# Attention: value sums and output projection exchange two PSUM banks with every group of heads

## The chip, the cores and the metric

The kernel runs on one core of one Trainium2 chip. The metric is the device time of one execution in microseconds (us). The engines are named as in the profile: PE is TensorE's matmul side, PEld its weight loads, DVE VectorE, ACT ScalarE, POOL GpSimd, SP the engine that issues DMAs. Each engine carries out its own instructions in the order of its queue.

## The reference, cut to what matters

One layer of a hybrid decoder: 1024 tokens, width 1024, float32. The normed input is projected; 8 heads of sparse attention in 2 groups and 4 heads of a gated recurrence follow; their outputs lie side by side and go through one output projection, which is added to the residual. A feed-forward block ends the layer. The change lies in the attention and the output projection that is woven into it:

```python
o = g[..., 0:1] * o_cmp + g[..., 1:2] * o_sel + g[..., 2:3] * o_win
...
mix = jnp.concatenate([o_nsa.astype(x.dtype), o_hgrn.astype(x.dtype)], axis=-1)
x = x + mix @ w_out[l]
```

`o_cmp`, `o_sel` and `o_win` are softmax(q k) v over compressed blocks, selected blocks and a window of 512 tokens. With 16 blocks of 64 tokens and 16 to be selected, the kernel takes all causal keys for `o_sel`.

## The kernel before

Attention goes through 8 blocks of 128 queries (`qb`), each with 2 groups of 4 heads (`g`), each with 2 branches (`b`: 0 all causal keys, 1 the window): 32 units. A unit has a scoring part and a value part, and the loop issues the scoring of one unit ahead of the values of the unit before it.

- `score`: for each of 4 heads, PE makes q k into a bank (L839 and L840 for the high and the low part of q, L842 for the mask). DVE takes the negated maximum (L847), ACT the exponential with its sum (L848), DVE the reciprocal of the sum (L849), and POOL multiplies by it and by the gate (L850), into `pbig`.
- `values`: for each block of 128 keys, PE transposes the 4 heads' weights (4 of L861) into a bank `ps_t`, ACT copies it as the high part `ph` (L863), DVE makes the low part (L864), and two matmuls of 512 columns, L865 with the high and L866 with the low part, add to the bank `o` of the group. Both units of a group add to one `o`.
- `finish`, after the second unit of a group, adds the compressed branch (L872 to L879) and reads `o` out: ACT L885 and L886 into `fold`, DVE L887 and L888 into `qtok`. From then on the bank is free.
- `prep` makes the queries of the next block ready: POOL writes them scaled (L775), PE transposes them (L781), ACT and DVE split them (L784, L785), and the compressed branch is scored (L790, L795).

The output projection is spread between the units. Each of its 32 tiles of 128 tokens x 512 columns needs 12 matmuls of 512 columns (L118 to L120) for one half of the inputs, `hgrn_out` for the recurrence's half and `nsa_out` for the attention's; DVE L497 adds the bank to `x1`, and the bank is free. A counter `load` decides after which unit the next tile is issued: the first one (`FILL` 6.5) comes at the fourth unit.

PSUM has 8 banks. Here 2 hold `ps_t`, 4 hold scores, and the last two are `a0` and `a1`: `o` always takes `a0` (`bank_o`), the projection always `a1` (`bank_f`). A tile that takes a bank waits until the reads of the tile before it in that bank are done.

The program text isn't the order on the engines: when the kernel is built, a scheduler lays each engine's instructions in an order by its own estimate of durations, within the dependences. A projection tile whose bank and data are ready is so spread, matmul by matmul, over places in PE's queue far ahead of where the text has it.

Of the kernel before, what the change touches and what calls it, by code (L numbers as in the profile page):

```python
# [8 lines left out]
F32 = mybir.dt.float32  # L9
# [9 lines left out]
P = 128  # L19
# [29 lines left out]
def hybrid_layer(ctx: ExitStack, tc: tile.TileContext, x, x_t, par, w_in, k_norm, pos_k, pos_v,  # L49
# [9 lines left out]
    ps = ctx.enter_context(tc.tile_pool(name="ps", bufs=1, space=PSUM))  # L59
# [45 lines left out]
    def rpage():  # L105
        return raw.tile([P, 1024], F32, name="rpage", tag="r")
# [392 lines left out]
    def mixhl():  # L499
        return rpage().bitcast(F32R).rearrange("p (two n) -> p two n", two=2)  # L500

    def bank_f():
        return ps.tile([P, 512], F32, name="a1", tag="a1", bufs=1)

    mixed = {}

# [7 lines left out]
    def hgrn_out(t, n, bank=bank_f):  # L514
        if n == 0 and t:
            mixed[t] = mix_parts(gmix[:, :, t * P:(t + 1) * P])
        out_tile(w_b, t, n, *mixed[t], bank)
# [212 lines left out]
    with tc.tile_pool(name="at", bufs=1) as at:  # L730
        g_bc = at.tile([P, D], F32, name="g_bc")
        nc.sync.dma_start(g_bc, norm_ffn[0:1, :].broadcast_to([P, D]))
        def nsa_out(t, n):
            if n == 0:
                mixed[t] = mix_parts(qtok[:, t].rearrange("p (c n) -> p c n", c=4))
            out_tile(w_t, t, n, *mixed[t], bank_f)
            if n == 1:
                nc.sync.dma_start(x1_d[t * P:(t + 1) * P, :], x1[:, t, :])
                rs2 = norm_stats(x1[:, t, :], rpage())
                if t == NT - 1:  # L740
                    g_last = rpage()
                    nc.sync.dma_start(g_last, norm_ffn[0:1, :].broadcast_to([P, D]))
                    V.scalar_tensor_tensor(x1[:, t, :], x1[:, t, :], rs2, g_last, op0=OP.mult, op1=OP.mult)
                    return
                A.activation(x1[:, t, :], x1[:, t, :], AF.Copy, scale=rs2)
                G.tensor_tensor(x1[:, t, :], x1[:, t, :], g_bc, op=OP.mult)
                if t >= 4:
                    G.tensor_tensor(x1[:, t, 0:512], x1[:, t, 0:512], x1[:, t - 4, 0:512], op=OP.subtract)
# [15 lines left out]
            return turns[1][:, 512 * (turns[0] - 2):512 * (turns[0] - 1)]  # L764

        def bank_o():
            return ps.tile([P, 512], F32, name="a0", tag="a0", bufs=1)

        def segs(n):
            return [(0, n)] if n <= 512 else [(0, n // 2), (n // 2, n // 2)]  # L770
# [127 lines left out]
        for i, u in enumerate(units + [None]):  # L898
# [8 lines left out]
            if pending:  # L907
                free[0] = i >= len(units) - 1
                (qb, g, b), kb0, wts = pending
                if b == 0:  # L910
                    o_bank[g] = bank_o()
                values(qb, g, b, kb0, wts, o_bank[g])
                if b == 1:
                    finish(qb, g, prepped[qb][1], o_bank[g])
                    if g == 1:
                        nq += [(qb, 0), (qb, 1)]
# [369 lines left out]
```

## Time and profile before

| what | us |
|---|---|
| median of 3 runs (1403.95, 1405.82, 1405.95) | 1405.82 |
| the profiled execution: its own time | 1406.47 |
| its span, first to last instruction | 1404.6 |
| PE busy in the span | 1371.6 |
| DVE busy | 1048.0 |
| ACT busy | 596.5 |
| POOL busy | 392.1 |

The attention with its woven-in projection lies between 394 and 742 us of the span. The profiled execution took 1.9 us more than its span, and its time is 0.65 us above the median. A busy PE need not be at its peak: a matmul that has begun and is held up counts as busy, so the distance from one start to the next tells more than busy time does. PEclk is the granted clock as a share of 2.4 GHz; the other level is 1.2 GHz, 0.5.

### The profile page before, as it was taken

The numbers are of one execution on the slowest core, as the hardware profiler recorded it, in microseconds if no ns is written. First come the engines' busy times: TensorE is split into PE (matmuls) and PEld (weight loads), VectorE is DVE, ScalarE is ACT, GpSimd is POOL, SyncE is SP. The second block draws the span as 40 slices with busy tenths as digits, with TensorE's granted clock in tenths as the row PEclk, the third lists the DMA queues.
The fourth block names the chain that finished last, engine by engine and source line by source line (L and its number), as shares of the span: only waits on it lengthen the run. The fifth ranks groups of instructions, "written<-read, shape, count | busy, mean of one in ns | idle before, by whom it ended". The sixth has DMA issues, their size and how long they took to land.

```text
span 1404.6 us, 19716 instructions
## 1 busy us (share of the span) xinstructions
PE 1371.6 (98%) x7092; PEld 1129.5 (80%) x7092; DVE 1048.0 (75%) x1893; ACT 596.5 (42%) x1153; POOL 392.1 (28%) x341
## 2 busy tenths in 40 slices
PE   9999999999999999999998999999999999999998
PEld 7888888989977777777776888888888888887787
DVE  5317888626788888888877888888888887689764
ACT  7323333323446666566654433333333333443332
POOL 0001111010044442344436433233233230158400
PEclk9999999999999999999999999999999999999999
DMA  8411110111220001000003333333333328887521
GB/s 324 127 45 31 31 31 28 54 31 46 94 88 1 1 1 61 31 16 31 16 16 105 96 101 97 112 98 113 113 112 99 106 98 294 327 300 269 171 97 55
DMA packets 108769, 135.72 MB, mean 97 GB/s; under 512 B 6112, under 2 KB 63872, under 8 KB 108672
## 3 DMA queue, kind: packets, MB, share of 16 engines
q1 hardware_dynamic: 108672, 134.46, 28.7%
q8 instruction: 56, 0.92, 0.3%
q14 instruction: 41, 0.34, 0.1%
HBM read 105.87 MB, written 28.57 MB: 96 GB/s over the span
## 4 chain that ended last, share of the span: by engine, by line
PE 82%; DVE 12%; ACT 2%; issue 2%; POOL 1%; DMA 1%; SPq 0%; ACTq 0%; POOLq 0%; DVEq 0%
PE bank L118 9%; PE bank L119 9%; PE bank L120 9%; PE a L118 8%; PE a L120 8%; PE a L119 8%; PE ps_t L119 4%; PE ps_t L120 4%; PE ps_t L118 4%; PE ps_t L861 3%; PE a L865 2%; DVE wop L112 2%; PE a L866 2%; PE ps_t L375 1%; PE ps_s L839 1%
## 5 line engine op out<-in xcount | busy, mean ns | idle before, releaser
L850 POOL TENSOR_SCALAR pbig<-pbig,den,gates 128x640 f32<-128x640 f32 (+7 forms) x128 | 103.9, 816 | 166.9 <-DVE den L849 146.9
L111 ACT ACTIVATE wop<-rpage 128x512 fp32r<-128x512 f32 x132 | 82.7, 630 | 156.9 <-PE bank L120 70.7
L112 DVE TENSOR_TENSOR wop<-rpage,wop 128x512 fp32r<-128x512 f32 x132 | 100.7, 765 | 14.6 <-ACT wop L111 12.7
L864 DVE TENSOR_TENSOR ph<-ps_t,ph 128x512 fp32r<-128x512 f32 x126 | 84.3, 683 | 18.5 <-ACT ph L863 17.6
L863 ACT ACTIVATE ph<-ps_t 128x512 fp32r<-128x512 f32 x126 | 72.7, 596 | 49.6 <-PE ps_t L861 39.7
L381 POOL TENSOR_TENSOR kp<-kp,fp 128x256 f32<-128x256 f32 x28 | 20.3, 725 | 232.8 <-PE bank L358 181.3
L861 PE MATMUL ps_t<-ident,pbig 128*128 128x128 f32 x504 | 78.7, 275 | 2.1 <-POOL pbig L850 2.1
L112 DVE TENSOR_TENSOR wop<-act_a,wop 128x512 fp32r<-128x512 f32 x48 | 46.8, 976 | 33.1 <-ACT wop L111 33.1
L861 PEld LDWEIGHTS ps_t<-ident,pbig 128*128 128x128 f32 x504 | 61.0, 141 | 11.9 <-POOL pbig L850 3.2
L1012 POOL TENSOR_TENSOR tmp<-tmp,rpage 128x512 f32<-128x512 f32 x21 | 31.3, 1488 | 140.6 <-DVE wop L112 140.6
L112 DVE TENSOR_TENSOR wlo<-wraw,whi 128x1024 fp32r<-128x1024 f32 (+2 forms) x27 | 32.0, 1188 | 46.0 <-PE a L120 19.3
L848 ACT ACTIVATE pbig<-ps_s,nm 128x640 f32<-128x640 f32 (+3 forms) x64 | 55.9, 875 | 24.1 <-DVE nm L847 19.0
L111 ACT ACTIVATE wop<-act_a 128x512 fp32r<-128x512 f32 x48 | 30.3, 631 | 82.8 <-PE bank L120 58.0
L118 PE MATMUL bank<-wop 128*128 128x512 f32 x165 | 65.3, 396 | 0.1
L119 PE MATMUL bank<-wop 128*128 128x512 f32 x165 | 65.2, 395 | 0.0
L120 PE MATMUL bank<-wop 128*128 128x512 f32 x165 | 65.1, 394 | 0.0
L847 DVE TENSOR_REDUCE nm<-ps_s 128x1 f32<-128x640 f32 (+3 forms) x64 | 58.1, 913 | 4.7 <-PE ps_s L842 3.0
L865 PE MATMUL a<-ph,kv 128*128 128x512 f32 x132 | 58.8, 445 | 2.2 <-ACT ph L863 1.4
L866 PE MATMUL a<-ph,kv 128*128 128x512 f32 x132 | 57.5, 436 | 2.9 <-DVE ph L864 1.8
L112 DVE TENSOR_TENSOR wop<-tmp,wop 128x512 fp32r<-128x512 f32 x42 | 43.6, 1039 | 20.6 <-ACT wop L111 19.9
L972 POOL TENSOR_TENSOR tmp<-rpage 128x512 f32<-128x512 f32 x20 | 26.1, 1306 | 115.2 <-DMA rpage<-in_w_gate_up_dram 115.2
L111 ACT ACTIVATE wop<-tmp 128x512 fp32r<-128x512 f32 x42 | 26.6, 633 | 70.2 <-POOL tmp L1012 37.5
(458 smaller groups left out, 4454.2 us busy)
## 6 DMA issues: line engine op xcount, KB each, us to landing
rpage<-in_w_gate_up_dram SPq DMA_DIRECT2D x86, 256.0 KB, 3.1
raws<-in_w_down_dram SPq DMA_DIRECT2D x35, 512.0 KB, 7.5
act_a<-act_d SPq DMA_DIRECT2D x12, 1024.0 KB, 6.4
act_d<-as SPq DMA_DIRECT2D x33, 256.0 KB, 2.2
act_e<-act_d SPq DMA_DIRECT2D x6, 1024.0 KB, 7.6
act_d<-tmp SPq DMA_DIRECT2D x22, 256.0 KB, 2.1
act_d<-th SPq DMA_DIRECT2D x22, 256.0 KB, 2.1
xn<-in_x_dram SPq DMA_DIRECT2D x8, 512.0 KB, 5.5
```

The costliest lines, as they stand in the source:

```text
L111: A.activation(hi, src, AF.Copy)
L112: V.tensor_tensor(lo, src, hi.bitcast(F32), op=OP.subtract)
L118: PE.matmul(o, ah, bh, start=first, stop=False, skip_group_check=chained)
L119: PE.matmul(o, ah, bl, start=False, stop=False, skip_group_check=chained)
L120: PE.matmul(o, al, bh, start=False, stop=last, skip_group_check=chained)
L847: V.tensor_reduce(nm, sv, axis=AX.XY, op=OP.max, negate=True)
L850: G.tensor_scalar(pp, pp, den, gates[:, qb, h * 3 + 1 + b:h * 3 + 2 + b], op0=OP.mult, op1=OP.mult)
L861: PE.transpose(pt[:, r * P:(r + 1) * P], wts[r][:, c0:c0 + P], ident)
L863: A.activation(ph[:, 0], pt, AF.Copy)
L864: V.tensor_tensor(ph[:, 1], pt, ph[:, 0].bitcast(F32), op=OP.subtract)
L865: PE.matmul(o, vst[b][:, kb, g, :], ph[:, 0], start=b == 0 and kb == kb0, stop=False)
L866: PE.matmul(o, vst[b][:, kb, g, :], ph[:, 1], start=False, stop=False)
```

## The change

`bank_o` now takes `a1` for the first group, `a0` for the second, and so on in turn; `bank_f` takes whichever of the two the latest group doesn't have, which is the bank of the group before.

```diff
+    side = [0]
+
     def bank_f():
-        return ps.tile([P, 512], F32, name="a1", tag="a1", bufs=1)
+
+        k = 1 - side[0]
+        return ps.tile([P, 512], F32, name=f"a{k}", tag=f"a{k}", bufs=1)
...
         def bank_o():
-            return ps.tile([P, 512], F32, name="a0", tag="a0", bufs=1)
+            side[0] ^= 1
+            return ps.tile([P, 512], F32, name=f"a{side[0]}", tag=f"a{side[0]}", bufs=1)
```

The same instructions run on every engine; their order changes on PE, DVE, ACT and POOL from the first unit of the attention on, and no longer after the attention. SP's order is the same. In the new text lines from 506 to 767 are 4 higher and later ones 5 higher: L790 of before is L795, L781 is L786, L839 is L844, L850 is L855, L775 is L780, L865 is L870.

PE at the first unit, before. `a1_3764` is the first projection tile that is woven in, `ps_t_3463` and `ps_t_3471` are the first queries' transpositions, `bank_3479` the compressed scores, `bank_3508` to `bank_3538` the four heads of the first unit:

```order
L781 MATMUL ps_t_3463<-ident_73,rpage_3461 128x128 x4
L118 MATMUL a1_3764<-whi_3327,rpage_3761 128x512
L781 MATMUL ps_t_3471<-ident_73,rpage_3461 128x128 x4
L119 MATMUL a1_3764<-wlo_3328,rpage_3761 128x512
...
L842 MATMUL bank_3528<-cmask_90,identb_78 128x128
L118 MATMUL a1_3764<-whi_3333,rpage_3761 128x512
L119 MATMUL a1_3764<-wlo_3334,rpage_3761 128x512
L120 MATMUL a1_3764<-whi_3333,rpage_3761 128x512
L118 MATMUL a1_3764<-whi_3339,rpage_3761 128x512
L119 MATMUL a1_3764<-wlo_3340,rpage_3761 128x512
L839 MATMUL bank_3538<-kv2_2683,q_3468 128x256
```

The same place with the change:

```order
L786 MATMUL ps_t_3463<-ident_73,rpage_3461 128x128 x4
L786 MATMUL ps_t_3471<-ident_73,rpage_3461 128x128 x4
L800 MATMUL bank_3479<-kc_st_91,q_3468 128x64
L844 MATMUL bank_3508<-kv2_2683,q_3468 128x256
...
L847 MATMUL bank_3528<-cmask_90,identb_78 128x128
L844 MATMUL bank_3538<-kv2_2683,q_3468 128x256
```

No projection matmul stands there any more. The tile now follows the end of the first group, whose sum is `a1_3588` (PE, with the change; `ps_t_3666` and `ps_t_3674` are the queries of the second block, `bank_3740` a score of the first, `bank_3778` and `bank_3788` scores of the second):

```order
L884 MATMUL a1_3588<-ph_3652,vc_up_93 128x2x128 x2
L786 MATMUL ps_t_3666<-ident_73,rpage_3664 128x128 x4
...
L844 MATMUL bank_3778<-kv2_2683,q_3671 128x256
L844 MATMUL bank_3788<-kv2_2683,q_3671 128x256
L118 MATMUL a1_3764<-whi_3327,rpage_3761 128x512
L119 MATMUL a1_3764<-wlo_3328,rpage_3761 128x512
L120 MATMUL a1_3764<-whi_3327,rpage_3761 128x512
L118 MATMUL a1_3764<-whi_3333,rpage_3761 128x512
L800 MATMUL bank_3682<-kc_st_91,q_3671 128x64 x7
```

All 12 of its matmuls moved there; before, all stood ahead of the end of the first group, and the first of the next tile, `a1_3904`, too. That next tile now follows the second group in the same way, and by the sixth group the same number of tiles has been issued as before.

POOL, before, at the second block's first unit: `den_3783` to `den_3813` are the sums of its four heads, and `rpage_4362` takes the scaled queries of the third block.

```order
L850 TENSOR_SCALAR pbig_3455<-pbig_3455,den_3783,gates_96 128x256
L850 TENSOR_SCALAR pbig_3455<-pbig_3455,den_3793,gates_96 128x256
L813 TENSOR_TENSOR pbig_3455<-pbig_3455,c_den_3702 128x512
L775 TENSOR_TENSOR rpage_4362<-qtok_101,rs_q_97 128x1024
L850 TENSOR_SCALAR pbig_3455<-pbig_3455,den_3803,gates_96 128x256
L850 TENSOR_SCALAR pbig_3455<-pbig_3455,den_3813,gates_96 128x256
```

With the change:

```order
L818 TENSOR_TENSOR pbig_3455<-pbig_3455,c_den_3702 128x512
L855 TENSOR_SCALAR pbig_3455<-pbig_3455,den_3783,gates_96 128x256
L855 TENSOR_SCALAR pbig_3455<-pbig_3455,den_3793,gates_96 128x256
L855 TENSOR_SCALAR pbig_3455<-pbig_3455,den_3803,gates_96 128x256
L855 TENSOR_SCALAR pbig_3455<-pbig_3455,den_3813,gates_96 128x256
...
L855 TENSOR_SCALAR pbig_3455<-pbig_3455,den_3943,gates_96 128x256
L780 TENSOR_TENSOR rpage_4362<-qtok_101,rs_q_97 128x1024
```

The scaled queries of the third block went from between the second and the third head to behind all four, and behind seven further heads.

## Rows read from the trace of the kernel before

**Rows 1.** The page: busy time of each engine; the chain that ended last, by engine.

```profile
PE 1371.6 (98%) x7092; PEld 1129.5 (80%) x7092; DVE 1048.0 (75%) x1893; ACT 596.5 (42%) x1153; POOL 392.1 (28%) x341
PE 82%; DVE 12%; ACT 2%; issue 2%; POOL 1%; DMA 1%; SPq 0%; ACTq 0%; POOLq 0%; DVEq 0%
```

**Rows 2.** Waits of PE, 394 to 742 us: total us, times, longest us.

```profile
PE ps_s L839 <- ACT pbig L848: 3.4, 6, 0.9
PE ps_t L861 <- POOL pbig L850: 2.1, 3, 1.4
PE a L866 <- DVE ph L864: 1.8, 5, 0.4
PE ps_t L657 <- DVE kd L650: 1.4, 1, 1.4
PE a L865 <- ACT ph L863: 1.4, 2, 1.2
PE a L866 <- DVE rs_t L129: 0.6, 1, 0.6
PE bank L795 <- ACT q L784: 0.5, 2, 0.3
PE a L866 <- DVE rs_v L125: 0.4, 1, 0.4
PE ps_t L781 <- ACT kv L658: 0.2, 1, 0.2
```

**Rows 3.** Busy us of PE, PEld, DVE, ACT, POOL by stretch, then PEclk.

```profile
394.00:407.00 13.00, 12.33 (x87) 10.05 (x86) 9.35 (x33) 7.40 (x26) 6.57 (x11) 1.00 0.11 42
421.00:425.00 4.00, 2.37 (x18) 1.74 (x16) 3.18 (x11) 3.17 (x11) 4.00 (x6) 1.00 0.00 0
425.00:428.40 3.40, 3.40 (x15) 2.92 (x14) 3.11 (x10) 2.31 (x9) 2.02 (x5) 0.50 0.01 2
440.00:480.00 40.00, 39.76 (x235) 30.29 (x235) 34.23 (x84) 25.87 (x68) 18.24 (x23) 1.00 0.00 1
561.60:565.00 3.40, 3.40 (x13) 2.61 (x12) 3.40 (x7) 0.99 (x2) 1.95 (x2) 0.50 0.00 0
```

**Rows 4.** The timeline of POOL: start us, us, operation, then idle and its releaser.

```profile
402.75 1.37 POOL L850 TENSOR_SCALAR pbig<-pbig,den,gates 128x128 f32<-128x128 f32 x3 [1.19 <-DVE den L849]
405.11 2.23 POOL L850 TENSOR_SCALAR pbig<-pbig,den,gates 128x128 f32<-128x128 f32 x5
421.25 1.89 POOL L775 TENSOR_TENSOR rpage<-qtok,rs_q 128x1024 f32<-128x1024 f32 x1
423.13 3.24 POOL L850 TENSOR_SCALAR pbig<-pbig,den,gates 128x256 f32<-128x256 f32 x6
```

**Rows 5.** The timeline of PE.

```profile
400.26 0.39 PE L119 MATMUL a<-wlo,rpage 128*128 128x512 f32 x1
400.49 0.40 PE L120 MATMUL a<-whi,rpage 128*128 128x512 f32 x1
...
404.17 0.33 PE L861 MATMUL ps_t<-ident,pbig 128*128 128x128 f32 x1
405.61 0.33 PE L861 MATMUL ps_t<-ident,pbig 128*128 128x128 f32 x1 [0.44 <-POOL pbig L850]
407.36 0.39 PE L861 MATMUL ps_t<-ident,pbig 128*128 128x128 f32 x2
423.74 0.33 PE L861 MATMUL ps_t<-ident,pbig 128*128 128x128 f32 x1 [1.42 <-POOL pbig L850]
424.27 0.66 PE L861 MATMUL ps_t<-ident,pbig 128*128 128x128 f32 x4 [0.21 <-POOL pbig L850]
```

**Rows 6.** The timelines of ACT and DVE: begin and end of a group's read-out.

```profile
410.39 0.38 ACT L885 ACTIVATE fold<-a 64x256 f32<-64x256 f32 x1
...
411.62 0.43 DVE L888 TENSOR_TENSOR qtok<-a,fold 64x256 f32<-64x256 f32 x1
```

**Rows 7.** The timeline of PE: the next group's first value matmul.

```profile
416.11 0.49 PE L865 MATMUL a<-ph,kv 128*128 128x512 f32 x1
```

**Rows 8.** The timeline of PE at the first and the last of 26 such places.

```profile
443.13 0.49 PE L861 MATMUL ps_t<-ident,pbig 128*128 128x128 f32 x3
443.63 0.50 PE L865 MATMUL a<-ph,kv 128*128 128x512 f32 x1
...
730.76 0.60 PE L861 MATMUL ps_t<-ident,pbig 128*128 128x128 f32 x4
731.12 0.48 PE L120 MATMUL a<-whi,rpage 128*128 128x512 f32 x1
731.61 0.50 PE L865 MATMUL a<-ph,kv 128*128 128x512 f32 x1
```

## The prediction

> **What bounds the kernel now.** I read the page first: PE is busy for 1371.6 us of the span and holds 82% of the chain that ended last [rows 1]. So the change pays only where it takes idle time or stretched steps out of PE's queue, or puts some in. Next I read PE's waits within the attention [rows 2]: 12 us in nine rows, most of them for the exponential (L848), for POOL's scaling (L850) and for the copies of the transposed weights (L863, L864). No row waits for L888, the end of a group's read-out, or for L497, the end of a projection's. The wait that the old banks could cause does not show.
>
> Then the stretches [rows 3]. From 394 to 407 us PE is busy for 12.33 of 13 us, but this is the stage in which the softmax of the first units sets the pace: the transposition at 404.17 starts just after POOL's three scalings end (402.75 + 1.37 = 404.12), the one at 405.61 has waited 0.44 for POOL, and the pair at 407.36 follows the end of five more (405.11 + 2.23 = 407.34) [rows 4, 5]. PE looks busy there because projection matmuls fill it. From 440 to 480 us PE is busy for 39.76 of 40 us [rows 3]: there PE sets the pace and a projection matmul costs its full step. In between, from 421 to 425, PE is busy for only 2.37 of 4 us, POOL for all 4, and in the 3.40 us that follow the granted clock is 0.50, the lower level of 1.2 GHz [rows 3].
>
> **The change, step by step.** The own time of the profiled execution is 1406.47, the median 1405.82; I make the sum against the former and take 0.65 off at the end.
>
> *The wait that it removes.* A group's first value matmul no longer waits for L888 of the group before, since it has the other bank. At the first hand-over L888 ends at 411.62 + 0.43 = 412.05 and the next L865 starts at 416.11, 4.06 us later [rows 6, 7]; its bank had long been free, and no row of PE's waits names it. I take 0. The most it can give: with the change two groups' first value matmuls stand right behind the last matmul of the group before, and could come earlier by the whole read-out, 1.66 us from the start of L885 at 410.39 to 412.05 [rows 6], so 3.3 us in all. The Trainium skill, Perfetto Trace Analysis, section Matmuls, says that independent matmul groups should rotate through different PSUM banks, so that the evacuation of one overlaps the next group's matmuls. By that rule the change should gain up to those 3.3 us; by the row, the evacuation was overlapped already. It is one of the rivals.
>
> *The first projection tile.* Its bank is now the one of the first group, so it has to wait for that group's read-out. Thirteen projection matmuls, the 12 of `a1_3764` and the first of `a1_3904`, leave the first group. A projection step is 0.23 us (400.26 to 400.49) [rows 5]: 3.0 us of filler. Since POOL and ACT set the pace there, PE idles in their place, and the same 13 steps run later, where PE is the bound. I give 0.3 us back, because scores that don't stand behind projection matmuls start a little sooner: **+2.7**. Bounds: +3.0, if nothing comes sooner, and +1.4, if the run of five matmuls ahead of the fourth head's scores had delayed the softmax by its whole 1.2 us and the wait of 0.44 before 405.61 goes too.
>
> *POOL's order.* The gap before 423.74 (1.42 us) and the one before 424.27 (0.21) are waits for L850 [rows 5]; on POOL the scaled queries, 1.89 us from 421.25, stand ahead of these scalings, which start at 423.13 [rows 4]. The change moves L775 behind all four heads and seven more. The transpositions also come about 3 us of PE work closer to their scores than before, so the chain of maximum, exponential and scaling will still be felt; I leave 0.5 us of the 1.63: **-1.1**. Bounds: -1.6 and +0.4.
>
> *The clock.* With 0.5 us in place of 1.63 I expect no fall after it. The 3.40 us at 0.50 did the work of 1.7 us [rows 3]: **-1.7**. Bounds: -1.7, and +1.7 if a new gap brings another fall. A second fall, 561.60 to 565.00 [rows 3], lies where PE's order is the same in both kernels; I keep it.
>
> *Value matmuls that follow their transpositions closely.* The copy by ACT lies between L861 and L865. Where PE has little to do in between, it waits within a step that counts as busy. At 731.61 L865 starts 0.49 us behind the projection matmul, not 0.23 [rows 5, 8]. I laid the median step of each pair of operations in this trace along both queues. Before, 26 of the 132 first value matmuls stand 0.6 to 0.8 us of PE work behind their last transposition, the first at 443.63, the last at 731.61, and they lost 0.22 us each [rows 8]. With the change 35 do, and three more stand still closer, because projection tiles now come in longer runs and less often between the two. At 9 x 0.22 + 3 x 0.3 less 0.2 for four places that move farther off: **+2.7**. Bounds: 0, if a wait at one place puts the next copies ahead and cancels, and +4, if the fold's copies (L874), of which three more stand close, wait as well.
>
> *Pairs.* The median steps of all pairs along the two queues add up to 0.5 us more with the change: **+0.5** (0 to +0.5). L497 and the read-outs only change places; DVE is busy for 34.23 of 40 us in the PE-bound stage [rows 3] and covers them. If that cover went, each would cost its 0.4 to 0.7 us once.
>
> Sum: 2.7 - 1.1 - 1.7 + 2.7 + 0.5 = +3.1, so 1409.6 for an execution like the profiled one and **1408.9** against the median.
>
> **The rivals.** *It washes out*, chance 0.33. The filler is only shifted, and what PE loses at the start it gets back: +1.4 for the start by its lower bound, -1.1 and -1.7 as above, half of the close followers (+1.4), +0.5: +0.5, 1406.3. For it: the fillers of 3.0 us are not lost, and the stage up to 440 us has other gaps to take them. Against it: the only large gap, at 423.74, takes 1.6 us and no more.
>
> *Faster*, chance 0.17, by one mechanism, the hand-over of the bank (the rule on rotating banks above). If the scheduler had spread the groups because of the bank, two groups now begin up to 1.66 us sooner each. That gives -3.3, with the gap and the clock -2.8, and the start +2.7; if the earlier starts also spare the close followers, -3.4 in all: 1402.4. It decides from a gain of some 2.5 us at these two places on. Against it: no wait for L888 in the rows.
>
> *A clock fall at the start*, chance 0.14, within the slower case. Without its 13 fillers PE is thinner from 394 to 407 us. If a fall like that of 425.00 follows, 1.7 us come on top: 1410.6. For it: 1.6 us of idle in 421 to 425 were enough [rows 3]. Against it: scores and transpositions still lie in every microsecond of the stretch.
>
> **How the numbers follow.** My forecast, with and without the fall at the start, holds 0.50 (0.36 and 0.14), no change 0.33, faster 0.17. A measurement of this kernel can tell about 0.2%, 2.8 us, from no change, so the forecast of +3.1 is just beyond it, and a part of the forecast's own spread (1407 to 1411) falls within it: slower 0.48, within 0.2% 0.36, faster 0.16. The range reaches from 1402.5, the faster rival, to 1411.5, the forecast with the fall and a little of the upper bounds.
>
> **What would show it.** In the profile of the changed kernel: PE less busy than 12.33 of 13 us in the first 13 us of the attention, by 1 to 3 us, with waits for POOL L850 or ACT there; no gap of over 1 us about 30 us into the attention, POOL's L780 behind the scalings, and a granted clock of 1.00 there; more starts of value matmuls (L870) held up behind L868; the first projection after the first group's L893. I am wrong if the first 13 us are as full as before, if a fall of the clock remains or a new one comes, or if the two close hand-overs shorten the attention by more than the start costs.

## The result, and the profile after

The changed kernel takes 1411.04 us (median of 5 runs, 1410.52 to 1414.56); the kernel before, on the same chip, 1403.95 (5 runs). The ratio is 1.0058, 95% interval [1.0047, 1.0070]. Profiled and timed again it took 1411.03 against 1403.69 (1.0052 [1.0038, 1.0065]). By the medians it is slower by 7.1 and 7.3 us, by the ratios by 8.1 and 7.3, where +3.1 was forecast. That the time itself lies within the range is luck: the kernel before also came out lower than its first three runs, at 1403.6 (median of 80 later runs) and not at 1405.82.

The page of the changed kernel: busy time by engine and the chain by engine.

```profile
PE 1378.2 (98%) x7092; PEld 1131.3 (80%) x7092; DVE 1051.0 (74%) x1893; ACT 595.5 (42%) x1153; POOL 392.3 (28%) x341
PE 81%; DVE 12%; ACT 3%; issue 2%; POOL 1%; DMA 0%; ACTq 0%; POOLq 0%; DVEq 0%
```

PE is busy for 6.6 us more with the same 7092 matmuls [rows 1], part of it because a slower clock stretches them. The second profile of each kernel (`e_after_again`, `e_again`, below) has fewer falls of the clock: there PE is busy for 1373.7 against 1369.8 us, in spans of 1409.8 and 1402.4. So about half of the loss hides within steps that count as busy, and the rest is idle time. PE's longest waits, 394 to 760 us:

```profile
PE ps_s L844 <- ACT pbig L853: 3.5, 6, 0.9
PE a L870 <- ACT ph L868: 1.9, 3, 1.3
PE a L871 <- DVE ph L869: 1.7, 5, 0.4
PE bank L800 <- ACT q L789: 1.3, 2, 0.8
PE ps_s L800 <- ACT q L789: 0.8, 1, 0.8
```

The scaling by POOL is gone from the list (in the second profile 0.4 us of it are left); the compressed scores' wait for the queries' copies (L800 for L789) has grown from 0.5 to 2.1 us [rows 2]. No row names a bank's release. The view of the read-out's last operation in the changed kernel says the same from the other side; its last line would list who waited for it, and is empty:

```profile
L893 DVE TENSOR_TENSOR qtok<-a,fold x16: 427/428/429, 412.4 to 747.5; 64x256 f32<-64x256 f32 x16
its engine sat idle before it (us, times) until:
who waited for it (us, times):
```

The stretches, with the columns of [rows 3]:

```profile
394.00:407.00 13.00, 12.19 (x73) 10.28 (x72) 8.90 (x32) 7.07 (x25) 5.81 (x9) 0.74 0.12 40
398.70:405.55 6.85, 6.79 (x33) 5.75 (x33) 4.64 (x20) 3.49 (x14) 3.25 (x7) 0.50 0.00 0
421.00:425.00 4.00, 3.88 (x25) 2.80 (x25) 3.20 (x13) 3.46 (x14) 3.40 (x7) 1.00 0.00 0
425.00:428.40 3.40, 3.40 (x21) 2.77 (x21) 3.12 (x10) 2.60 (x9) 1.30 (x3) 1.00 0.01 2
440.00:480.00 40.00, 39.08 (x227) 29.76 (x226) 32.15 (x77) 24.39 (x64) 18.89 (x24) 1.00 0.00 1
```

In 421 to 425 PE is busy for 3.88 of 4 us, not 2.37, and no fall of the clock follows. There is one at the start instead, twice as long (6.85 us at 0.50); it makes 12.19 busy us out of fewer matmuls. And where PE was all but full, 440 to 480, it now does 227 matmuls in place of 235, with 1.3% fewer columns in all.

POOL in the changed kernel: the scaled queries (L780) stand behind the scalings, as foretold [rows 4].

```profile
422.04 2.69 POOL L855 TENSOR_SCALAR pbig<-pbig,den,gates 128x256 f32<-128x256 f32 x5 [0.34 <-DVE den L854]
...
430.46 1.90 POOL L780 TENSOR_TENSOR rpage<-qtok,rs_q 128x1024 f32<-128x1024 f32 x1
```

What was lost shows best at the second block's queries. PE in the changed kernel:

```profile
410.79 1.04 PE L786 MATMUL ps_t<-ident,rpage 128*128 128x128 f32 x8
411.66 0.22 PE L847 MATMUL bank<-cmask,identb 128*128 128x128 bf16 x1
412.67 0.30 PE L800 MATMUL bank<-kc_st,q 128*128 128x64 f32 x1 [0.79 <-ACT q L789]
412.81 0.49 PE L844 MATMUL bank<-kv,q 128*128 128x256 f32 x2
413.13 0.39 PE L118 MATMUL a<-whi,rpage 128*128 128x512 f32 x1
413.36 0.40 PE L119 MATMUL a<-wlo,rpage 128*128 128x512 f32 x1
```

The queries are transposed, the copy by ACT takes its time, PE idles for 0.79 us, and only then come the projection's matmuls, three of which would have fitted into the gap.

### The profile page after: what moved, and what is told of

It reads as the page before. It is cut to its first block, busy times and chain, and to the rows that moved or that the text cites. A ratio compares the mean times of both kernels' runs of the same rounds, so it can differ in the third digit from the quotient of the medians.

```text
span 1412.4 us, 19720 instructions
## 1 busy us (share of the span) xinstructions
PE 1378.2 (98%) x7092; PEld 1131.3 (80%) x7092; DVE 1051.0 (74%) x1893; ACT 595.5 (42%) x1153; POOL 392.3 (28%) x341
## 4 chain that ended last, share of the span: by engine, by line
PE 81%; DVE 12%; ACT 3%; issue 2%; POOL 1%; DMA 0%; ACTq 0%; POOLq 0%; DVEq 0%
PE bank L118 9%; PE bank L119 9%; PE bank L120 9%; PE a L120 8%; PE a L118 8%; PE a L119 8%; PE ps_t L119 4%; PE ps_t L120 4%; PE ps_t L118 4%; PE ps_t L866 3%; PE a L870 2%; DVE wop L112 2%; PE a L871 2%; PE ps_t L375 1%; DVE nm L852 1%
## 5 line engine op out<-in xcount | busy, mean ns | idle before, releaser
L855 POOL TENSOR_SCALAR pbig<-pbig,den,gates 128x640 f32<-128x640 f32 (+7 forms) x128 | 102.7, 807 | 165.5 <-DVE den L854 143.5
L112 DVE TENSOR_TENSOR wop<-rpage,wop 128x512 fp32r<-128x512 f32 x132 | 101.0, 767 | 14.8 <-ACT wop L111 12.8
L868 ACT ACTIVATE ph<-ps_t 128x512 fp32r<-128x512 f32 x126 | 73.0, 595 | 51.1 <-PE ps_t L866 42.7
L118 PE MATMUL bank<-wop 128*128 128x512 f32 x165 | 65.3, 396 | 0.2 <-DVE res L1179 0.2
L120 PE MATMUL bank<-wop 128*128 128x512 f32 x165 | 65.1, 395 | 0.0
L870 PE MATMUL a<-ph,kv 128*128 128x512 f32 x132 | 59.7, 452 | 3.3 <-ACT ph L868 1.9
```

Of the source, the lines that this page charges most:

```text
L112: V.tensor_tensor(lo, src, hi.bitcast(F32), op=OP.subtract)
L118: PE.matmul(o, ah, bh, start=first, stop=False, skip_group_check=chained)
L120: PE.matmul(o, al, bh, start=False, stop=last, skip_group_check=chained)
L855: G.tensor_scalar(pp, pp, den, gates[:, qb, h * 3 + 1 + b:h * 3 + 2 + b], op0=OP.mult, op1=OP.mult)
L868: A.activation(ph[:, 0], pt, AF.Copy)
L870: PE.matmul(o, vst[b][:, kb, g, :], ph[:, 0], start=b == 0 and kb == kb0, stop=False)
```

## The experiments

Three theories at first. **A**: the projection's tiles have to wait for a read-out before the scheduler may place them, so they no longer stand where PE has nothing else; the loss comes at a few places (in its first form: the first group, the seventh to ninth, the last three). **B**: the fall of the clock at the start is the whole loss. **C**: every exchange of roles costs the same. A fourth, **H**, was that the hand-over of the bank is worth something by itself.

Six kernels exchange roles for some groups only. All count groups in `bank_o`, have `bank_f` as in the change, and differ in the line that sets `side` (each has one of the six); lines from 768 of before on are 7 higher:

```diff
         def bank_o():
-            return ps.tile([P, 512], F32, name="a0", tag="a0", bufs=1)
+            groups[0] += 1
+            side[0] = 1 if groups[0] == 1 else 0                       # e_first
+            side[0] = side[0] ^ 1 if groups[0] <= 6 else 0             # e_early
+            side[0] = 0 if groups[0] <= 6 else side[0] ^ 1             # e_late
+            side[0] = side[0] ^ 1 if 7 <= groups[0] <= 9 else 0        # e_mid
+            side[0] = side[0] ^ 1 if 10 <= groups[0] <= 13 else 0      # e_ten
+            side[0] = side[0] ^ 1 if groups[0] >= 13 else 0            # e_last
+            return ps.tile([P, 512], F32, name=f"a{side[0]}", tag=f"a{side[0]}", bufs=1)
```

**Only the first group** (`e_first`). 

> Only the first group's value sum takes a1, all later ones a0, the projection always the other bank: only the first woven-in projection tile has to wait for a group's read-out. Theory A (the loss is made of lost filler at the start, and of later stages where projection tiles come in long runs): the first 20 us of the attention lose some 3.6 us as with the whole change, POOL's scaled queries move behind the second block's scalings and give back 1.4 to 2.8, nothing is lost later: 1 to 2.5 us over the kernel before. Theory B (the clock fall at the start is the whole loss): 7 us over. Theory C (the exchange at every group costs): about 0.5 us over (one exchange of 16).

Measured: 1405.73, 1.0012 [1.0004, 1.0021], +1.8 us. A's size; too little for B.

**The first six groups** (`e_early`). 

> The first six groups exchange banks as in the change, the other ten keep the roles of before. Theory A: the losses and the gains of the first 100 us of the attention stay (in the two traces +3.6, -1.4, +1.8, -0.6, +1.5 by stretches of 20 us), those behind go: 4 to 5.5 us over the kernel before. Theory B: 7 us over. Theory C: 6 of 16 exchanges, 2.7 us over.

Measured: 1409.58, 1.0040 [1.0028, 1.0052], +5.6 us. As A has it, and too much for C.

**The last ten groups** (`e_late`). 

> The first six groups keep the roles of before, the last ten exchange. Theory A: the start is as before, with its gap and its clock fall near 423 us; only the losses behind 100 us stay: 1.5 to 3 us over the kernel before. Theory B: no difference from before, within 1 us. Theory C: 10 of 16 exchanges, 4.4 us over.

Measured: 1408.28, 1.0037 [1.0023, 1.0050], +4.4 us to +5.2 by the ratio. A's 1.5 to 3 is too low, C's share fits here. Early and late together make some 10 us, more than the whole change: the parts don't add up.

**The changed kernel with idle filler at the start** (`e_dummy`): 12 matmuls of 512 columns into the free bank, their results unused.

```diff
+                if i == 2:
+                    spare = ps.tile([P, 512], F32, name="a0", tag="a0", bufs=1)
+                    for _ in range(12):
+                        PE.matmul(spare, kst[0, 0][:, 0:P], kst[0, 0][:, 0:512], start=True, stop=True)
```

> The changed kernel with 12 further matmuls of 512 columns into the bank that is idle during the first group; nothing reads their result. They stand where the first projection tile stood before. Theory A: they keep PE busy, so the clock does not fall near 399 us, but they do no work that is needed later: the attention gains 0.5 to 2.5 us on the changed kernel, and stays 4.5 to 6.5 us over the kernel before. Theory B: without the clock fall the loss is gone, at most 2 us over the kernel before. If the matmuls cost their own time, 2.8 us more than the changed kernel.

Measured: 1410.81, 1.0052 [1.0039, 1.0065]. Its profile has no fall of the clock in the whole attention. The first 13 us of the attention in its stretches:

```profile
394.50:407.50 13.00, 12.55 (x90) 10.09 (x88) 9.06 (x33) 7.63 (x27) 6.88 (x11) 1.00 0.13 40
```

PE is full again and the clock is at 1.00, and the time is that of the changed kernel within 0.3 us: B falls. A's own forecast, 0.5 to 2.5 us less than the changed kernel, did not come either. The run shows the start's price too. The second group ends 28.95 us after the attention's first matmul, against 28.75 without the 12 idle matmuls (`e_after_again`, below). Twelve matmuls that cost 2.8 us where PE sets the pace (12 x 0.23) cost 0.2 us here. That is what the kernel before got for its first projection tile.

**The values alternate, the projection doesn't share** (`e_three` and `e_three_alt6`). With three banks of scores in place of four up to the fourth block, one bank is free. The control leaves it empty, the other gives it to the value sums of groups 2, 4 and 6.

```diff
-        return pool[0].tile([P, 512], F32, name="bank", tag="s", bufs=4)
+        return pool[0].tile([P, 512], F32, name="bank", tag="s", bufs=scores[0])
...
+            turn_o[0] += 1
+            if turn_o[0] not in (2, 4, 6):
+                return ps.tile([P, 512], F32, name="a0", tag="a0", bufs=1)
+            return pool[0].tile([P, 512], F32, name="v1", tag="v1", bufs=1)
```

> The kernel before with three banks of scores in place of four for the first four blocks of queries, so that a bank is free there; values keep a0, the projection keeps a1. This is only the control for the next run. All theories: somewhat slower than before, by 0 to 6 us, since a score has to wait more often for the exponential of the score three ahead of it.

> The control with the freed bank given to the value sums of the second, fourth and sixth group; the projection keeps a1, so the values alternate between two banks and the projection shares neither. Instructions stand in the same order on every engine as in the control. H (a hand-over of the bank from group to group costs time, so alternating is worth something by itself): 0.5 to 3.3 us faster than the control, in the first six groups. A (the read-out was always done in time; the loss comes only from what the projection does when it has to share): within 0.5 us of the control, segment by segment.

Measured: 1404.89 and 1404.74, with the same ratio to the kernel before, 1.0005 [0.9997, 1.0014]. PE at the attention's first matmul and at the end of the sixth group, in the control (lines 7 higher than before) and in the other (12 higher):

```profile
394.66 0.27 PE L797 MATMUL bank<-cmask,identb 128*128 128x256 bf16 x1
...
478.49 0.40 PE L886 MATMUL a<-ph,vc_up 128*128 128x256 f32 x2
```

```profile
394.21 0.27 PE L802 MATMUL bank<-cmask,identb 128*128 128x256 bf16 x1
...
478.12 0.40 PE L891 MATMUL v<-ph,vc_up 128*128 128x256 f32 x2
```

83.83 and 83.91 us from the one to the other, with the same order on every engine. H falls: a bank of one's own for the next group is worth nothing in these six groups. And alternating costs nothing there as long as the projection keeps its bank. So it is the sharing that costs; that later groups behave in the same way was not tested by itself.

**POOL's order alone** (`e_scale`): the kernel before with the scaled queries of the third block issued one step earlier (`scale` is the scaling, taken out of `prep`).

```diff
+                if u == (0, 1, 1):
+                    scale(2)
```

> The kernel before with one edit: the scaled queries of the third block are issued at the second unit of the first block's second group, so that on POOL they no longer stand between the scalings of the second block's first unit. Roles of the banks as before. If the term for POOL's order was right: the gap of 1.4 us on PE about 30 us into the attention is gone, with it the clock fall behind it, 1.1 to 3.3 us faster than before up to the end of the sixth group. If the time that PE gains there is taken up by the next wait for the exponential: within 0.5 us of before. If the fall comes somewhere else instead: no faster than before in time, though the gap is gone.

Measured: 1404.74, 1.0011 [1.0001, 1.0020], +1.2 us. POOL and PE at that place (L776 is L775 of before, L857 is L850, L868 is L861, L846 is L839):

```profile
422.67 1.74 POOL L857 TENSOR_SCALAR pbig<-pbig,den,gates 128x256 f32<-128x256 f32 x3
424.38 1.90 POOL L776 TENSOR_TENSOR rpage<-qtok,rs_q 128x1024 f32<-128x1024 f32 x1
```

```profile
424.51 1.04 PE L868 MATMUL ps_t<-ident,pbig 128*128 128x128 f32 x8
426.16 0.39 PE L846 MATMUL bank<-kv,q 128*128 128x256 f32 x1 [0.30 <-ACT pbig L855]
```

The edit does not move the tile that it was meant for. L775 runs once a block, and the one in the gap at 421.25 is the fourth of them (382.84, 386.96, 396.60, 421.25): `rpage_4362` holds the queries of the fourth block, not of the third, as the section on the change has it. Issuing the third block's scaling earlier made the scheduler lay POOL's queue anew, and in that order the fourth block's scaling stands behind the four heads. What the gap costs can be read from it all the same.

The gap of 1.42 us is gone, and the third group takes 11.8 us, against 12.8 in an execution of before's order without a fall: -1.0, close to the -1.1 of the forecast. But the second group ends 0.5 us later, all of it lost in the first group. In this profile a fall, from 394.63 on, lies across the attention's first 1.5 us; whether the 0.5 us come from it or from the new order was not told apart.

The whole is no gain, as the last of the three outcomes has it, but the fall is only a part of the reason: the attention's first matmul comes at 396.54 us, not at 394.65. A scaling on POOL now runs while DVE casts keys, the cast takes 2.13 us in place of 0.43, and PE waits for the keys 1.7 us longer. DVE, POOL and PE in `e_scale`, then DVE and PE in the kernel before:

```profile
391.80 2.13 DVE L649 CAST kd<-kraw 128x512 fp32r<-128x512 f32 x1
391.76 1.90 POOL L776 TENSOR_TENSOR rpage<-qtok,rs_q 128x1024 f32<-128x1024 f32 x1 [3.54 <-PE bank L120]
394.81 1.94 PE L657 MATMUL ps_t<-ident,kd 128*128 128x128 f32 x8 [3.13 <-DVE kd L650]
```

```profile
392.45 0.43 DVE L649 CAST kd<-kraw 128x512 fp32r<-128x512 f32 x1
393.75 1.07 PE L657 MATMUL ps_t<-ident,kd 128*128 128x128 f32 x8 [1.43 <-DVE kd L650]
```

That the scaling holds up the cast is read from the two standing side by side; no run was made for it.

**Groups 7 to 9** (`e_mid`). 

> Only the seventh to ninth group exchange roles, all others keep a0 for the values and a1 for the projection. A (the loss sits at three places, at the first group, around the seventh to ninth and at the last three): +2.9 us against before, nearly all of it between the end of the sixth group and the end of the ninth, so 1406.5 to 1407.5. C (each exchange costs the same share of 7 us): three of sixteen, +1.3 us. D (a shift of the projection at one place is paid wherever the order on PE next differs, not at the place itself): 0 to +1 us in that stretch, and the rest later or not at all.

Measured: 1406.41, 1.0020 [1.0011, 1.0028], +2.9 us: A's size. In the profile the woven part (the attention's first matmul to the last one of its projection) is 2.0 us longer than before, 1.8 of it in these groups, so D falls.

**Groups 10 to 13** (`e_ten`). 

> Only the tenth to thirteenth group exchange roles. A (the loss sits at the first group, around the seventh to ninth and at the last three): 0 to +0.6 us against before. C (each exchange costs the same share of 7 us): +1.8 to +2.2 us.

Measured: 1411.00, 1.0051 [1.0039, 1.0064], +7.4 us, as much as the whole change. Both A, in its form of three places, and C fall. Groups 10 to 13 themselves take no longer (112.0 us, before 111.8, with one fall of the clock in each); the last three, whose roles are before's, take 94.7 us in place of 86.3. Of this, rows account for one part. A projection matmul waits for the low part of its inputs, DVE L516, and a fall of the clock begins 1 us later, at 702.18:

```profile
701.15 0.50 PE L120 MATMUL a<-whi,rpage 128*128 128x512 f32 x1 [1.32 <-DVE rpage L516]
```

No such wait is in the kernel before or in the changed one. The tile was laid where PE comes to it before its own inputs are ready.

**The last four groups** (`e_last`). 

> Only the last four groups exchange roles. A: +2.4 us against before, all of it behind the end of the thirteenth group. C: +1.8 us. Knock-on (what the last groups lost in the changed kernel was only passed on from the earlier ones): under +0.8 us.

Measured: 1407.60, 1.0023 [1.0013, 1.0033]: +3.2 us by the ratio, +4.0 by the medians. In the profile the woven part is 2.1 us longer than in `e_again` (next), which has the same two falls, 1.9 of it behind the thirteenth group. A and C both pass; the knock-on does not.

**The kernel before, once more** (`e_again`). 

> The kernel before, unedited, profiled once more. What is asked is whether the fall of the clock about 30 us into the attention belongs to this order of instructions, as the prediction had it (then it is there again, with the gap of 1.4 us ahead of it, and the first three groups end 41.5 us after the attention's first matmul), or comes in some executions only (then the gap is there without a fall, and the three groups end near 40.0). Time within 0.1% of before.

Measured: 1403.08, 0.9997 [0.9987, 1.0007]. Its fall is there again. Now three executions whose order is before's at this place: `e_again`, `e_late` and `e_ten`, each with the stretch of the gap and the one behind it.

```profile
421.40:425.40 4.00, 2.36 (x19) 1.73 (x18) 3.18 (x10) 3.20 (x11) 4.00 (x6) 1.00 0.00 0
425.40:428.90 3.50, 3.50 (x16) 2.93 (x15) 3.17 (x11) 2.47 (x9) 2.19 (x5) 0.51 0.01 2
```

```profile
421.00:425.00 4.00, 2.38 (x19) 1.85 (x17) 3.18 (x12) 3.52 (x12) 4.00 (x6) 1.00 0.00 0
424.70:428.10 3.40, 3.40 (x23) 2.83 (x23) 3.07 (x11) 2.37 (x9) 2.07 (x5) 1.00 0.01 2
```

```profile
421.00:425.00 4.00, 2.38 (x20) 1.85 (x19) 3.17 (x11) 3.60 (x12) 4.00 (x6) 1.00 0.00 0
424.60:428.00 3.40, 3.40 (x24) 2.84 (x23) 3.08 (x10) 2.37 (x9) 2.09 (x5) 1.00 0.01 2
```

The same gap, and a fall behind it in the first alone. Of the six profiles with this order four have the fall (before, `e_again`, `e_mid`, `e_last`). It costs 1.54 us: the third group ends at 41.49 us with it and at 39.95 without.

**The changed kernel, once more** (`e_after_again`). 

> The changed kernel, unedited, profiled once more. If the loss is one of order (the projection's matmuls stand in other places, and what they hid lies open): the woven part lasts 360 to 363 us from the attention's first matmul to the last matmul of its projection, 5 to 8 us more than in the kernel before, with or without a fall of the clock at the start, and each of the first six groups ends within 0.3 us of the first profile apart from what the falls cost. If the fall at the start made the loss: 3 us less than in the first profile where it is missing. Time within 0.1% of the first measurement of the changed kernel.

Measured: 1411.03, 1.0052 [1.0038, 1.0065]. There is no fall within the attention:

```profile
394.30:407.30 13.00, 10.83 (x80) 8.47 (x79) 9.30 (x34) 7.89 (x28) 6.88 (x11) 1.00 0.12 40
421.00:425.00 4.00, 3.89 (x28) 3.02 (x29) 3.13 (x13) 3.44 (x13) 2.69 (x5) 1.00 0.00 0
```

At full clock the emptier start shows bare: 10.83 us busy of 13, not 12.33 [rows 3]. The woven part lasts 360.3 us, against 362.4 in the first profile and 354.7 in the kernel before. The loss is one of order.

## Why the prediction was wrong

Executions without falls give a clean account of the woven part. The order of before is taken from profiles in which that stretch has no fall (groups 1 to 6 from `e_late`, 10 to 13 from `e_scale`, where PE's order is before's, the others from the kernel before itself), the changed one from `e_after_again`. Times are those between the starts of the groups' last matmuls, L879 (L884 with the change):

| groups | before, us | changed, us | difference |
|---|---|---|---|
| 1 to 6 | 84.5 | 87.1 | +2.6 |
| 7 to 9 | 59.6 | 62.5 | +2.9 |
| 10 to 13 | 110.7 | 111.1 | +0.4 |
| 14 to 16 | 86.3 | 88.8 | +2.5 |
| behind them, to the last projection matmul | 10.9 | 10.9 | 0.0 |

+8.3 in all, before rounding. The attention's first matmul and the end of the sixth group, in `e_late` (L886 is L879 of before) and in `e_after_again`; a line that stands for two matmuls begins with the first, and the table counts to the second, 0.12 us later:

```profile
394.30 0.27 PE L797 MATMUL bank<-cmask,identb 128*128 128x256 bf16 x1
...
478.71 0.40 PE L886 MATMUL a<-ph,vc_up 128*128 128x256 f32 x2
```

```profile
394.61 0.27 PE L795 MATMUL bank<-cmask,identb 128*128 128x256 bf16 x1
...
481.58 0.40 PE L884 MATMUL a<-ph,vc_up 128*128 128x256 f32 x2
```

(Nine matmuls of scores moved from ahead of the sixth group's end to behind it, so the first two rows are best read together: +5.5.)

To see which steps grew, I took the median of each pair of neighbouring operations over 13 profiles and summed what each step of PE took beyond it, by the operation that started late, steps within falls apart; kernel before against `e_after_again`: first value matmuls +3.2, scores +3.8 (2.1 of it in the first three groups), compressed scores +1.5 (1.0 in the first three), transpositions -0.9, projection matmuls -0.8, all others +0.3; the medians themselves +1.4. That is +8.5; the two falls that before's profile has and the other has not take off 2.9, and the rest is the +5.6 between the two profiles. The sum is firm, the split is not: over all 14 profiles, with pairs told apart by line and shape, the same four are first value matmuls +3.4, scores +3.1, compressed scores +1.5 and medians +1.7; with the tile as well +3.1, +4.8, +1.3 and +0.7.

The table has no falls, so the forecast to set beside its +8.3 is the sum without the clock's -1.7: +4.8. Point by point:

- **The removed wait, 0**: right. No one waits for L893, and the alternating alone (`e_three_alt6`) changed nothing. The Trainium skill, Perfetto Trace Analysis, section Matmuls, has independent matmul groups rotate through PSUM banks; here that changed nothing where the second bank was free (83.83 and 83.91 us for six groups), and lost 7 us where it was another consumer's.
- **The first projection tile, +2.7**: right, at its upper bound of +3.0. At full clock the first group ends 15.42 us after the attention's first matmul with the thirteen projection matmuls (`e_late`) and 15.39 without them (`e_after_again`): nothing came sooner, and 13 x 0.23 us of work were left for later. `e_dummy` agrees: 2.6 of 2.8 us of filler are free there.
- **POOL's order, -1.1**: right in place; -1.0 in the third group of `e_scale`, -0.9 in the transpositions as a whole.
- **The clock, -1.7**: mis-sized. The fall at 425 is gone, but it cost 1.54 us and had come in only four executions of six, so it was worth 1.0 and not 1.7; the same 1.6 us of idle stood ahead of it in all six. The rival's fall at the start did come, in the first profile and in `e_early`, not in `e_first`, `e_dummy` or `e_after_again`, and cost 1.0 us at most (the sixth group ends at 88.06 with 6.8 us of it, at 87.09 without).
- **Close followers, +2.7**: right for what it counted, +3.2 (+3.1 and +3.4 by the other two ways).
- **Pairs, +0.5**: +1.4 (+0.7 and +1.7), beyond the upper bound.

The step that failed is the term for value matmuls that follow their transpositions closely, as the only price behind the start; the clock's -1.7, taken in full from one profile, comes second. The term counted one kind of cover: projection matmuls between a transposition of weights and the value matmul behind it. The same matmuls also cover the copies of the queries (L784) ahead of the compressed scores, and the exponentials (L848) that free the banks of scores. Nothing in the sum stood for these beyond the first tile. They measure +1.7 for scores and +0.5 for compressed scores behind the third group, and the larger medians add 0.9: 3.1 us, or 2.0 to 3.1 by the other ways of telling pairs apart. For the compressed scores PE's waits say the same without medians, 2.1 us in place of 0.5. For the scores it is this account alone, and no run took their share by itself. One such place, the last block's queries, in the kernel before (`e_again`) and in the changed one:

```profile
651.27 0.60 PE L781 MATMUL ps_t<-ident,rpage 128*128 128x128 f32 x4
...
652.13 0.39 PE L119 MATMUL a<-wlo,rpage 128*128 128x512 f32 x1
652.36 0.40 PE L120 MATMUL a<-whi,rpage 128*128 128x512 f32 x1
...
652.95 0.60 PE L781 MATMUL ps_t<-ident,rpage 128*128 128x128 f32 x4
653.30 0.28 PE L795 MATMUL ps_s<-kc_st,q 128*128 128x64 f32 x1
```

```profile
657.30 0.93 PE L786 MATMUL ps_t<-ident,rpage 128*128 128x128 f32 x7
659.03 0.30 PE L800 MATMUL ps_s<-kc_st,q 128*128 128x64 f32 x1 [0.81 <-ACT q L789]
659.31 0.47 PE L118 MATMUL a<-whi,rpage 128*128 128x512 f32 x1
659.62 0.40 PE L119 MATMUL a<-wlo,rpage 128*128 128x512 f32 x1
```

Before, the two halves of the transpositions stand apart, with two projection matmuls and the fold between them, and the compressed scores follow without a wait. After, the first transposition stands within the fold and the other seven together behind it, the copy lies open, and the projection comes behind that. Counted along PE's queue up to the sixteenth group, the same 317 matmuls of L118 to L120 stand in 126 places in place of 143, and 55 of them, not 16, in runs of six or more.

That 7.1 us were measured and not the 8.3 of the table fits the falls: the kernel before has more of them in its attention (two in each of its two profiles; the changed kernel's two have two and none). The granted clock of the timed runs agrees: its mean is 0.9964 over 80 runs of the kernel before and 0.9972 over the ten of the changed one, that is 10.0 and 7.9 us at the lower level in each execution. At 1.54 us for 3.41 us the difference is worth an estimated 0.9 us.

What stays open: why each order costs what it does. Seven ways of exchanging roles cost 1.8 to 7.4 us, neither by their number nor by their place; the sharing makes the scheduler lay another order from there on, and none of these was better than before's. That the order is the price, and nothing else that comes with the sharing, is inferred: no wait names a bank, and no run had the changed order with the old banks. For `e_ten` the wait for L516 and the fall behind it explain some 3 of its 8.4 us in the last groups; the rest was not taken apart. None of the edited kernels was faster than the one before.

## What to carry to other kernels

A stream of matmuls without urgency, woven in as filler, was worth most here with a bank of its own: let it share a bank with work that has due times, and no one may ever wait for that bank, yet the filler moves out of the gaps into runs. When a change moves filler, list every kind of wait that it covered (each engine's copies ahead of each kind of matmul), and price each in the order of the changed kernel, not only the one that shows in the waits. Before you build on a fall of the clock in one profile, see whether it is there in a second. And before an edit is to move one instruction, see which of its instances stands at the place: `e_scale` moved another.

## What was not expected of the hardware

Behind the same gap (PE busy 2.36 to 2.38 of 4 us) the clock fell in four executions and stayed in two. The Trainium skill, TensorE: Matmul & The Clock Gate, section "What's actually happening", says that the chip's look at PE's activity runs free of the kernel, which agrees; no run here shows it apart. A fall of the clock costs by what sets the pace: 3.41 us at 1.2 GHz cost 1.54 us in the third group, and 6.8 us of it at the start, where ACT and POOL set the pace, 1.0. And a DVE operation can stretch beside one of POOL's: in `e_scale` a cast took 2.13 us in place of 0.43 beside a scaling of 1.90 us, in the kernel before an operation of L129 took 1.76 us beside another (from 387.12 and 386.96 on), where the next of L129, with POOL idle, took 0.17.
